# Narrow matmuls of a hybrid decoder trunk laid on alternating column halves of TensorE

## The chip, the cores and the metric

The kernel runs on one core of a Trainium2 chip. The metric is the device time of one execution in microseconds (us). Times come from repeated executions, and one further execution was recorded by the hardware profiler; all rows below are of that one.

## The reference, cut to what matters

One decoder layer for 512 positions, width 1024, all float32. A combined projection of the normalised input feeds three token mixers (sparse attention, spatial gating, RWKV-7), whose outputs are merged and projected. Three small pieces of it are touched here.

```python
# compression of keys and of values (kv = 0, 1): 31 windows of 32 positions, two groups
blk = kv[:, idx] + pe[:, None, :]
hid = silu(einsum('bnlgd,ldh->bngh', blk, w1))        # the first layer
out = einsum('bngh,hd->bngd', hid, w2)
# RWKV-7, 8 heads of 64 channels
kk = kkf / maximum(sqrt(sum(kkf * kkf, axis=-1)), 1e-12)   # a sum of squares per position and head
state = state * d_t + sa * b_t + v_t * k_t                 # the recurrence
y = einsum('bhij,bhj->bhi', state, r_t)                    # its output
y = (y - mean(y)) * rsqrt(var(y) + GN_EPS) * lnx_g + lnx_b # normalised per position and head
```

## The kernel before, in words

Large projections are made with operands split into a high and a low part (`wload` at lines 68 to 79 loads a block of weights, ScalarE makes the high part `wh`, GpSimd or VectorE the low part `wl`); three matmuls into `mm_ps` per piece of the contraction stand for one. These are the bulk of TensorE's work, and they run all the way through. The touched pieces are plain float32 matmuls, each of which is two instructions in the trace; a transpose is one.

All loops are unrolled in Python. The framework orders the instructions of each engine when the kernel is built: it goes by its own estimate of when operands are ready, and among ready instructions takes the one that stands first in the program. On the chip each engine then runs its list in that order.

* First compression layer (loop over `kv` from line 286): 16 matmuls accumulate into `hid`, 64 partitions high, once for keys and once for values. The stationary operand is `blk[:, l, :]` (128 rows by 64 columns), the moving one `w1t[:, l, :]` (128 columns). `hid` has one buffer, so the values' group comes after the keys' result has been read. Each group is followed by tanh, a product, a transpose (`slp`) and the second layer (`pk`).
* Sums of squares (lines 375 to 377): for each of 4 position tiles and 4 channel tiles a matmul with 128x128 stationary columns of `sq` and 8 moving columns of `hind`, into `ss_ps`.
* The recurrence, 8 chunks of 64 positions (`c`, from line 529). Heads lie in 4 pairs `q` with parity `e`; `own[e]` is partitions 0 to 63 or 64 to 127. Per chunk there are 8 matmuls each for `r_ps`, `u_ps` and `st_ps`, whose outputs go to `own[e]` with `e` alternating, and two sets of 8 for the output `Yp`: one of 64x64 operands (from `rt`, whose rows are `own[e]`), one of 128 rows (from `Gt`). Before the change `Yp` is one tile per head parity, and both sets of a chunk write the partition half `ur` that belongs to the chunk's parity `u`.
* Every second chunk the output of two chunks is normalised (`mu`, `yc`, `ysq`, `va`) and transposed by 4 TensorE transposes of 128x128 into `yt_ps`, from which `vt` is updated.

Projections of other parts (`su`, `sv`, `sz`, `sg`, `rz`, `nz`) stand later in the program and fill TensorE between the steps of the recurrence; `canch` (last output matmul of each chunk) anchors two of them.

Of the kernel before, what the change touches and what calls it, by code (L numbers as in the profile page):

```python
# [9 lines left out]
F32 = mybir.dt.float32  # L10
R = mybir.dt.float32r
BF = mybir.dt.bfloat16
AF = mybir.ActivationFunctionType
OP = mybir.AluOpType
AX = mybir.AxisListType
# [29 lines left out]
def hybrid_kernel(ctx, tc, x, p, norm_g, w_in, cmp_w1, cmp_w2, cmp_pe, sg_ln_g, sg_ln_b, sg_w, sg_b,  # L45
# [3 lines left out]
    V, S, G, PE, SY = nc.vector, nc.scalar, nc.gpsimd, nc.tensor, nc.sync  # L49
    x, p, w_in = x[0], p[0, 0], w_in[0]  # L50
# [9 lines left out]
    def mm(o, a, b, start, stop, **kw):  # L60
        return PE.matmul(o, a, b, start=start, stop=stop, **kw).ins  # L61
# [31 lines left out]
    ident = const.tile([128, 128], F32, name="ident")  # L93
# [28 lines left out]
    mhalf = const.tile([128, 32], F32, name="mhalf")  # L122
# [5 lines left out]
    hind = const.tile([128, 4, 8], F32, name="hind")  # L128
# [81 lines left out]
    for t in range(4):  # L210
# [6 lines left out]
        for a in range(2):  # L217
            ks = slice(4 * a, 4 * a + 4)
            ps = xps.tile([128, 4, 128], F32, tag="xt", name="xt_ps")
# [10 lines left out]
    kt_, rt = AR[:, 0], AR[:, 1]  # L230
# [13 lines left out]
    cpp = cp_ctx.enter_context(tc.tile_pool(name="cpp", bufs=1))  # L244
    cps = cp_ctx.enter_context(tc.tile_pool(name="cps", bufs=1, space=PSUM))
# [5 lines left out]
    for half in range(2):  # L251
        c0 = half * 256
        for kv in range(2):
            hs, ls = wkc[kv]
            ps = pmm.tile([128, 512], F32, tag="mm", name="mm_ps")
# [27 lines left out]
    for kv in range(2):  # L283
        for d in range(2):
            SY.dma_start(w2t[:, kv, d * 64:d * 64 + 64], cmp_w2[0, kv])
    for kv in range(2):
        w1t = cpp.tile([128, 16, 128], F32, tag="w1t", name="w1t", bufs=2)
        for lh in range(2):
            SY.dma_start(w1t[lh * 64:lh * 64 + 64], cmp_w1[0, kv, lh * 16:lh * 16 + 16].rearrange("l d h -> d l h"))
        blk = cpp.tile([128, 16, 64], F32, tag="blk", name="blk", bufs=2)  # L290
        src = kc2[:, kv].rearrange("p g (n l) -> p l (g n)", l=16)
        V.tensor_tensor(blk, src, pc("pe", kv * 16, 16).unsqueeze(2).to_broadcast([128, 16, 64]), OP.add)
        hid = cps.tile([64, 128], F32, tag="hid", name="hid")
        for l in range(16):
            mm(hid, blk[:, l, :], w1t[:, l, :], l == 0, l == 15)
        th = cpp.tile([64, 128], F32, tag="th", name="th")
        S.activation(th, hid, AF.Tanh, scale=0.5)
        V.scalar_tensor_tensor(th, th, 1.0, hid, op0=OP.add, op1=OP.mult)
        slp = cps.tile([128, 64], F32, tag="slp", name="slp")
        PE.transpose(slp, th, ident[0:64, 0:64])  # L300
        sl = cpp.tile([128, 2, 4, 32], F32, tag="sl", name="sl")
        if kv == 0:
            sl = sl[:, 0, 0:2, :].rearrange("p g n -> p (g n)")
            V.tensor_copy(sl, slp)
            pk = cps.tile([128, 64], F32, tag="pk", name="pk")
            mm(pk, w2t[:, 0, :], sl, True, True)
            pk2 = pk.rearrange("p (g n) -> p g n", g=2)
            S.activation(kcst[:, :, 0, :], pk2, AF.Copy, scale=0.5)
            V.scalar_tensor_tensor(kcst[:, :, 1, :], pk2, 0.5, f(kcst[:, :, 0, :]), op0=OP.mult, op1=OP.subtract)
        else:  # L310
            V.tensor_copy(sl, slp.rearrange("p (g n) -> p g n", g=2).unsqueeze(2).to_broadcast([128, 2, 4, 32]))
            for g in range(2):
                pk = cps.tile([128, 64], F32, tag="pk", name="pk")
                mm(pk, sl[:, g].rearrange("p a n -> p (a n)"), w2t[:, 1, 0:64], True, True)
                S.activation(vcst[:, g, 0:64], pk, AF.Copy, scale=0.5)
                V.scalar_tensor_tensor(vcst[:, g, 64:128], pk, 0.5, f(vcst[:, g, 0:64]),
                                       op0=OP.mult, op1=OP.subtract)
# [25 lines left out]
    Gt = rp.tile([128, 2, 4, 8, 2, 64], F32, name="Gt")  # L343
    SV = rp.tile([128, 8, 2, 4, 64], F32, name="SV")
# [7 lines left out]
    rps = pr_ctx.enter_context(tc.tile_pool(name="rps", bufs=1, space=PSUM))  # L352
# [4 lines left out]
    for i, src in ((0, rk_w2), (1, rk_a2)):  # L357
        a, o = (slice(0, 64), slice(64, 128)) if i == 0 else (slice(64, 128), slice(0, 64))
# [11 lines left out]
    sqs = []  # L370
# [3 lines left out]
        sqs.append(sq)  # L374
    for t in range(4):
        for q in range(4):
            mm(ss_ps[:, t, :], sqs[q][:, t * 128:(t + 1) * 128], hind[:, q, :], q == 0, q == 3)
    rin = pr.tile([128, 4, 8], F32, name="rin")
    V.tensor_scalar(rin, ss_ps, 1e-24, None, op0=OP.max)
    G.tensor_tensor(rin, rin, mhalf.rearrange("p (a b) -> p a b", b=8), OP.pow)  # L380
# [147 lines left out]
    own = [slice(0, 64), slice(64, 128)]  # L528
    for c in range(8):
        cs = slice(c * 64, c * 64 + 64)  # L530
        u = c % 2
        ur = slice(u * 64, u * 64 + 64)
        if u == 0:
            Yp = [rps.tile([128, 4, 64], F32, tag=f"y{e}", name="Yp") for e in range(2)]
        r_ps = rps.tile([128, 4, 64], F32, tag="ch", name="r_ps", bufs=2)
        for q in range(4):
            for e in range(2):
                mm(r_ps[own[e], q, :], Gt[:, e, q, c, 0, :], SV[:, c, e, q, :], True, True)
        for q in range(4):
            for e in range(2):  # L540
                mm(Yp[e][ur, q, :], rt[own[e], q, cs], SV[own[e], c, e, q, :], q == 0, False,
                   skip_group_check=True)
        r_sb = iv.tile([128, 4, 64], F32, tag="r_sb", name="r_sb", bufs=2)
        S.copy(r_sb, r_ps)
        u_ps = rps.tile([128, 4, 64], F32, tag="ch", name="u_ps", bufs=2)
        for q in range(4):
            for e in range(2):
                mm(u_ps[own[e], q, :], XT[own[e], q * 8 + c, :], r_sb[own[e], q, :], True, True)
        V.tensor_copy(SV[own[0], c, 0], u_ps[own[0]])
        S.copy(SV[own[1], c, 1], u_ps[own[1]])  # L550
        if c < 7:
            s_ps = rps.tile([128, 4, 64], F32, tag="ch", name="st_ps", bufs=2)
            for q in range(4):
                for e in range(2):
                    mm(s_ps[own[e], q, :], BKt[:, c, q, e, :], SV[:, c, e, q, :], True, True)
            tn = iv.tile([128, 4, 64], F32, tag="tn", name="tn", bufs=2)
            dbc = Dt[:, :, c:c + 1].to_broadcast([128, 4, 64])
            if c == 0:
                V.tensor_tensor(tn, s_ps, dbc, OP.mult)
            else:  # L560
                V.tensor_tensor(tn, s_ps, sn, OP.add)
                V.tensor_tensor(tn, tn, dbc, OP.mult)
            sn = tn
            V.tensor_copy(SV[own[0], c + 1, 0], tn[own[0]])
            S.copy(SV[own[1], c + 1, 1], tn[own[1]])
        for q in range(4):
            for e in range(2):
                last = mm(Yp[e][ur, q, :], Gt[:, e, q, c, 1, :], SV[:, c, e, q, :], False, q == 3,
                          skip_group_check=True)
        canch.append(last)  # L570
        if u == 1:
            t = c // 2
            ts = slice(t * 128, (t + 1) * 128)
            mu = iv.tile([128, 4, 2], F32, tag="mu", name="mu", bufs=2)
            yc = iv.tile([128, 4, 2, 64], F32, tag="yc", name="yc", bufs=2)
            for e in range(2):
                V.tensor_reduce(mu[:, :, e], Yp[e], axis=AX.X, op=OP.add)
            V.tensor_scalar(mu, mu, 1.0 / 64, None, op0=OP.mult)
            for e in range(2):
                V.tensor_tensor(yc[:, :, e, :], Yp[e], mu[:, :, e].unsqueeze(2).to_broadcast([128, 4, 64]),  # L580
                                OP.subtract)
            ysq = iv.tile([128, 4, 2, 64], F32, tag="ysq", name="ysq", bufs=1)
            S.activation(ysq, yc, AF.Square)
            va = iv.tile([128, 4, 2], F32, tag="va", name="va", bufs=2)
            V.tensor_reduce(va, ysq, axis=AX.X, op=OP.add)
            V.tensor_scalar(va, va, 1.0 / 64, 64e-5, op0=OP.mult, op1=OP.add)
            G.tensor_tensor(va, va, mhalf[:, 0:8].rearrange("p (a b) -> p a b", b=2), OP.pow)
            V.tensor_tensor(yc, yc, va.unsqueeze(3).to_broadcast([128, 4, 2, 64]), OP.mult)
            ps = rps.tile([128, 4, 128], F32, tag="g", name="yt_ps")
            for q in range(4):  # L590
                PE.transpose(ps[:, q, :], yc[:, q].rearrange("p e i -> p (e i)"), ident)
            for q in range(4):
                V.scalar_tensor_tensor(vt[:, q, ts], ps[:, q, :], pc("lnx_g", q), vt[:, q, ts],
                                       op0=OP.mult, op1=OP.add)
# [391 lines left out]
```

## Time and profile before

| | |
|---|---|
| runs of the kernel, us | 1015.65, 767.99, 767.72 (median 767.99) |
| the profiled execution, us | 766.05 |
| its span, first to last instruction, us | 764.3 |
| TensorE busy, us | 729.1 |
| mean granted TensorE clock | 0.994 |

The profiled execution is 1.75 us longer than its span and 1.94 us shorter than the median. In the timeline rows below the first number is the start in us, the second how long the group of like instructions lasted. Matmuls overlap, so what one costs the engine is read from the distance between starts, not from its duration.

### The profile page before, as it was taken

Reading aid. Unit: us, or ns where it says so; the run is one execution under the profiler, and the core shown is the slowest. Engines: PE = TensorE matmul, PEld = TensorE weight load, DVE = VectorE, ACT = ScalarE, POOL = GpSimd, SP = SyncE. Lnnn points to the kernel's source line nnn. Section 1 sums busy time; section 2 is a strip of 40 time slices with the busy share of each in tenths; the row PEclk is TensorE's granted clock in tenths of the full one; section 3 lists DMA queues with packets and bytes.
Section 4 is the critical chain, followed back from the end, with each engine's and each line's share of the span. In section 5 each row is a group of like instructions: output and inputs, shape, how many; then the busy total and the mean of one; then the engine's idle time right before and its main releaser. Section 6 shows DMA issues by size and latency. Waiting matters only on the chain.

```text
span 764.3 us, 13017 instructions
## 1 busy us (share of the span) xinstructions
PE 729.1 (95%) x4910; PEld 617.9 (81%) x4910; DVE 398.3 (52%) x748; ACT 353.8 (46%) x744; POOL 325.7 (43%) x304
## 2 busy tenths in 40 slices
PE   4899999999999899999899999989999999999996
PEld 4888877899877888778777777867877888998995
DVE  6531387758826642444649455477664222226335
ACT  6455455543362333333456564466654333226453
POOL 6444541120245443423644334534344666255563
PEclk9999999999999999999999999999999999999999
DMA  6843222125535453444533222311116433222222
GB/s 200 189 112 89 56 69 62 36 90 153 147 107 196 112 148 89 115 153 146 155 86 110 70 56 56 82 29 42 42 42 218 141 96 106 88 92 75 84 69 110
DMA packets 106688, 78.71 MB, mean 103 GB/s; under 512 B 5569, under 2 KB 97282, under 8 KB 106626
## 3 DMA queue, kind: packets, MB, share of 16 engines
q1 hardware_dynamic: 105890, 75.27, 34.5%
q10 hardware_dynamic: 736, 2.63, 0.8%
q8 instruction: 38, 0.62, 0.3%
q14 instruction: 24, 0.20, 0.1%
HBM read 67.91 MB, written 9.96 MB: 102 GB/s over the span
## 4 chain that ended last, share of the span: by engine, by line
PE 82%; DVE 7%; DMA 4%; ACT 3%; issue 2%; POOL 1%; SPq 1%; ACTq 0%; POOLq 0%; DVEq 0%
PE mm_ps L61 64%; PE s_ps L61 3%; PE o_ps L61 2%; PE g_ps L61 2%; PE p_ps L850 2%; PE Yp L61 1%; PE hid L61 1%; DMA vn<-dr_sv 1%; DMA xs__129<-in_x_dram 1%; DMA zs<-dr_nz 1%; DVE vn L662 1%; DVE mx L836 1%; ACT wh L77 1%; DVE vn L660 1%; PE mx_ps L61 1%
## 5 line engine op out<-in xcount | busy, mean ns | idle before, releaser
L78 POOL TENSOR_TENSOR wl<-wr,wh 128x512 fp32r<-128x512 f32 (+1 forms) x168 | 224.5, 1344 | 306.4 <-ACT wh L77 288.1
L77 ACT CAST wh<-wr 128x512 fp32r<-128x512 f32 (+1 forms) x194 | 119.3, 620 | 173.9 <-PE mm_ps L61 114.2
L61 PE MATMUL mm_ps<-hH,wh 128*128 128x512 f32 (+1 forms) x440 | 174.4, 396 | 6.4 <-ACT gate L736 2.7
L61 PE MATMUL mm_ps<-hH,wl 128*128 128x512 f32 (+1 forms) x440 | 172.7, 393 | 0.4 <-DVE wl L78 0.4
L61 PE MATMUL mm_ps<-hL,wh 128*128 128x512 f32 (+1 forms) x440 | 172.7, 393 | 0.0
L61 PEld LDWEIGHTS mm_ps<-hH,wh 128*128 128x128 f32 x440 | 83.6, 190 | 25.0 <-ACT gate L736 3.4
L61 PEld LDWEIGHTS mm_ps<-hH,wl 128*128 128x128 f32 x440 | 83.4, 190 | 18.6 <-DVE wl L78 0.6
L61 PEld LDWEIGHTS mm_ps<-hL,wh 128*128 128x128 f32 x440 | 83.4, 190 | 16.9 <-issue 0.4
L61 PE MATMUL mm_ps<-wh,hH 128*128 128x256 f32 (+1 forms) x224 | 64.2, 288 | 4.5 <-DVE st L625 3.3
L61 PE MATMUL mm_ps<-wh,hL 128*128 128x256 f32 (+1 forms) x224 | 64.0, 287 | 0.0
L61 PE MATMUL mm_ps<-wl,hH 128*128 128x256 f32 (+1 forms) x224 | 63.7, 285 | 0.0
L61 PEld LDWEIGHTS mm_ps<-wh,hH 128*128 128x128 f32 x224 | 42.0, 188 | 6.4 <-DVE st L625 3.5
L61 PEld LDWEIGHTS mm_ps<-wl,hH 128*128 128x128 f32 x224 | 42.1, 188 | 0.6
L61 PEld LDWEIGHTS mm_ps<-wh,hL 128*128 128x128 f32 x224 | 42.1, 188 | 0.6 <-issue 0.2
L854 DVE TENSOR_TENSOR pl<-p_ps,ph 128x512 fp32r<-128x512 f32 x40 | 27.1, 684 | 26.8 <-ACT ph L853 26.6
L61 PE MATMUL mm_ps<-ysH,wh 128*128 128x512 f32 x96 | 38.6, 402 | 0.3 <-ACT ysH L705 0.3
L61 PE MATMUL mm_ps<-ysL,wh 128*128 128x512 f32 x96 | 38.4, 400 | 0.2 <-DVE ysL L706 0.2
L61 PE MATMUL mm_ps<-ysH,wl 128*128 128x512 f32 x96 | 38.2, 398 | 0.0
L837 ACT ACTIVATE P<-s_ps,mx 128x512 f32<-128x512 f32 (+3 forms) x64 | 33.4, 531 | 7.9 <-DVE mx L836 5.5
L61 PE MATMUL mm_ps<-wh,mH 128*128 128x256 f32 x128 | 36.2, 287 | 0.6 <-DVE x L899 0.6
L61 PE MATMUL mm_ps<-wl,hT 128*128 128x256 f32 x128 | 35.8, 281 | 0.0
L61 PE MATMUL mm_ps<-wh,hT 128*128 128x256 f32 x128 | 35.8, 285 | 0.0
(336 smaller groups left out, 1450.4 us busy)
## 6 DMA issues: line engine op xcount, KB each, us to landing
wr<-in_w_in_dram SPq DMA_DIRECT2D x130, 256.0 KB
wr<-in_w_branch_dram SPq DMA_DIRECT2D x24, 256.0 KB
wr<-in_w_o_dram SPq DMA_DIRECT2D x16, 256.0 KB
wr<-in_w_ple_gate_dram SPq DMA_DIRECT2D x16, 256.0 KB
xs__129<-in_x_dram SPq DMA_DIRECT2D x4, 512.0 KB
w1t<-in_cmp_w_dram SPq DMA_DIRECT2D x4, 512.0 KB
x<-in_x_dram ACTq DMA_DIRECT2D x4, 512.0 KB
out_dram<-x SPq DMA_DIRECT2D x8, 256.0 KB
```

Of the source, the lines that this page charges most:

```text
L61: return PE.matmul(o, a, b, start=start, stop=stop, **kw).ins
L77: S.copy(h[:, :m], raw[:, :m])
L78: ph_["l"].tensor_tensor(l[:, :m], raw[:, :m], f(h[:, :m]), OP.subtract)
L660: V.tensor_scalar(vn[:, t, :], vn[:, t, :], mv[:, t, 0:1], rs4[:, t:t + 1], op0=OP.subtract, op1=OP.mult)
L662: V.tensor_tensor(vn[:, t, :], vn[:, t, :], lnb, OP.add)
L836: V.tensor_reduce(mx[:, hh:hh + 1], s_ps[:, :W], axis=AX.X, op=OP.max, negate=True)
L837: S.activation(P[:, hh, :W], s_ps[:, :W], AF.Exp, bias=mx[:, hh:hh + 1], accum_out=sm[:, hh:hh + 1])
L850: PE.transpose(p_ps[:, hh * 128:hh * 128 + 128], P[:, hh, kt * 128:kt * 128 + 128], ident)
L854: V.tensor_tensor(pl, p_ps, f(ph), OP.subtract)
```

## The change

The layout of four pieces on TensorE changes, with the layout of the normalisation that follows one of them.

* First compression layer: `hid` is 128 partitions high, keys in the lower half and values in the upper; the two accumulations are interleaved, step by step, in one loop. Tanh and product are done once for both, and one 128x128 transpose takes the place of two. `sl` has a buffer for each.
* Sums of squares: each matmul is cut into two of 64 stationary columns, whose outputs are the lower and the upper partition half of `ss_ps`; 32 matmuls instead of 16.
* Recurrence output: `Yp` is one tile per chunk parity, and the output of a head goes to `own[e]`.
* Transpose of the output: instead of 4 transposes per two chunks, 16 matmuls of 64x64 with a piece of the identity as moving operand.

```diff
-        hid = cps.tile([64, 128], F32, tag="hid", name="hid")
-        for l in range(16):
-            mm(hid, blk[:, l, :], w1t[:, l, :], l == 0, l == 15)
-        th = cpp.tile([64, 128], F32, tag="th", name="th")
-        S.activation(th, hid, AF.Tanh, scale=0.5)
-        V.scalar_tensor_tensor(th, th, 1.0, hid, op0=OP.add, op1=OP.mult)
-        slp = cps.tile([128, 64], F32, tag="slp", name="slp")
-        PE.transpose(slp, th, ident[0:64, 0:64])
-        sl = cpp.tile([128, 2, 4, 32], F32, tag="sl", name="sl")
+        w1.append(w1t)
+        bl.append(blk)
+
+    hid = cps.tile([128, 128], F32, tag="hid", name="hid")
+    for l in range(16):
+        for kv in range(2):
+            mm(hid[kv * 64:kv * 64 + 64], bl[kv][:, l, :], w1[kv][:, l, :], l == 0, l == 15, skip_group_check=True)
+    th = cpp.tile([128, 128], F32, tag="th", name="th")
+    S.activation(th, hid, AF.Tanh, scale=0.5)
+    V.scalar_tensor_tensor(th, th, 1.0, hid, op0=OP.add, op1=OP.mult)
+    slp2 = cps.tile([128, 128], F32, tag="slp", name="slp")
+    PE.transpose(slp2, th, ident)
+    for kv in range(2):
+        slp = slp2[:, kv * 64:kv * 64 + 64]
+        sl = cpp.tile([128, 2, 4, 32], F32, tag=f"sl{kv}", name="sl")
...
-            mm(ss_ps[:, t, :], sqs[q][:, t * 128:(t + 1) * 128], hind[:, q, :], q == 0, q == 3)
+            for u in range(2):
+                mm(ss_ps[u * 64:u * 64 + 64, t, :], sqs[q][:, t * 128 + u * 64:t * 128 + u * 64 + 64], hind[:, q, :],
+                   q == 0, q == 3, skip_group_check=True)
...
-            Yp = [rps.tile([128, 4, 64], F32, tag=f"y{e}", name="Yp") for e in range(2)]
+            Yp = [rps.tile([128, 4, 64], F32, tag=f"y{a}", name="Yp") for a in range(2)]
...
-                mm(Yp[e][ur, q, :], rt[own[e], q, cs], SV[own[e], c, e, q, :], q == 0, False,
+                mm(Yp[u][own[e], q, :], rt[own[e], q, cs], SV[own[e], c, e, q, :], q == 0, False,
                    skip_group_check=True)
...
-                last = mm(Yp[e][ur, q, :], Gt[:, e, q, c, 1, :], SV[:, c, e, q, :], False, q == 3,
+                last = mm(Yp[u][own[e], q, :], Gt[:, e, q, c, 1, :], SV[:, c, e, q, :], False, q == 3,
                           skip_group_check=True)
...
-            mu = iv.tile([128, 4, 2], F32, tag="mu", name="mu", bufs=2)
-            yc = iv.tile([128, 4, 2, 64], F32, tag="yc", name="yc", bufs=2)
-            for e in range(2):
-                V.tensor_reduce(mu[:, :, e], Yp[e], axis=AX.X, op=OP.add)
+            mu = iv.tile([128, 2, 4], F32, tag="mu", name="mu", bufs=2)
+            yc = iv.tile([128, 2, 4, 64], F32, tag="yc", name="yc", bufs=2)
+            for a in range(2):
+                V.tensor_reduce(mu[:, a, :], Yp[a], axis=AX.X, op=OP.add)
...
             for q in range(4):
-                PE.transpose(ps[:, q, :], yc[:, q].rearrange("p e i -> p (e i)"), ident)
+                for a in range(2):
+                    for e in range(2):
+                        mm(ps[own[e], q, a * 64:a * 64 + 64], yc[own[e], a, q, :], ident[own[e], own[e]], True, True)
```

The lines left out change the layouts of `yc`, `ysq` and `va` in the same way, with the same number of instructions of the same sizes.

## Rows read from the trace of the kernel before

**Rows 1.** The page: busy time of each engine.
```profile
PE 729.1 (95%) x4910; PEld 617.9 (81%) x4910; DVE 398.3 (52%) x748; ACT 353.8 (46%) x744; POOL 325.7 (43%) x304
```
**Rows 2.** Windows: stretch, length, busy us of PE, PEld, DVE, ACT, POOL; clock, DMA.
```profile
34.00:46.00 12.00, 12.00 (x72) 9.83 (x71) 4.53 (x7) 5.82 (x11) 4.07 (x4) 1.00 0.89 200
...
240.00:260.00 20.00, 16.66 (x209) 15.33 (x210) 14.96 (x22) 5.85 (x13) 11.65 (x8) 1.00 0.23 62
```
**Rows 3.** Timeline of TensorE in a chunk: two sets that alternate already.
```profile
240.15 0.69 PE L61 MATMUL r_ps<-SV,Gt 128*64 128x64 f32 x16
240.76 0.68 PE L61 MATMUL Yp<-SV,AR 64*64 64x64 f32 x16
241.38 0.38 PE L61 MATMUL mm_ps<-wh,hH 128*128 128x256 f32 x1
```
**Rows 4.** Timeline of TensorE, chunk 4: the 128-row output set and the next group.
```profile
294.58 1.10 PE L61 MATMUL Yp<-SV,Gt 128*64 128x64 f32 x16
295.61 0.70 PE L61 MATMUL mx_ps<-vn,wsT 128*128 128x256 f32 x2
```
**Rows 5.** Timeline of TensorE around the two groups of the first compression layer.
```profile
36.13 3.71 PE L61 MATMUL hid<-w1t,blk 128*64 128x128 f32 x32
39.77 0.51 PE L61 MATMUL mm_ps<-hH,wh 128*128 128x512 f32 x1
...
45.07 0.27 PE L300 MATMUL slp<-ident,th 64*128 64x64 f32 x1
45.27 3.49 PE L61 MATMUL hid<-w1t,blk 128*64 128x128 f32 x30
```
**Rows 6.** Timeline of TensorE: 64-row matmuls with 128 moving columns, alternating and not.
```profile
110.69 1.16 PE L61 MATMUL g_ps<-AR,bk 64*128 64x128 f32 x16
111.78 0.66 PE L467 MATMUL bk_ps<-ident,bk 128*128 128x128 f32 x4
...
120.64 1.16 PE L61 MATMUL g_ps<-AR,bk 64*128 64x128 f32 x8
121.73 0.66 PE L401 MATMUL v_ps<-ident,vt 128*128 128x128 f32 x4
```
**Rows 7.** Timeline of TensorE around the sums of squares.
```profile
70.78 0.73 PE L61 MATMUL ss_ps<-hind,sq 128*128 128x8 f32 x6
71.37 0.60 PE L387 MATMUL hi_ps<-ident,hind 128*8 128x128 f32 x4
...
74.83 2.96 PE L61 MATMUL ss_ps<-hind,sq 128*128 128x8 f32 x26
77.64 0.48 PE L61 MATMUL mm_ps<-hH,wh 128*128 128x512 f32 x1
```
**Rows 8.** Windows just after the sums of squares (columns as in Rows 2).
```profile
79.00:80.00 1.00, 1.00 (x3) 0.74 (x3) 0.00 (x0) 0.00 (x0) 1.00 (x1) 0.50 0.06 18
```
**Rows 9.** Timeline of TensorE around that stretch: first, tenth and eleventh of the large matmuls.
```profile
78.44 0.51 PE L61 MATMUL mm_ps<-hH,wh 128*128 128x512 f32 x1
...
82.08 0.39 PE L61 MATMUL mm_ps<-hH,wh 128*128 128x512 f32 x1
82.31 0.39 PE L61 MATMUL mm_ps<-hL,wh 128*128 128x512 f32 x1
```
**Rows 10.** Timeline of TensorE, last chunk: half of the 64-row output set.
```profile
337.59 0.68 PE L61 MATMUL Yp<-SV,AR 64*64 64x64 f32 x8
338.19 0.66 PE L676 MATMUL ut_ps<-ident,us 128*128 128x128 f32 x4
```
**Rows 11.** Timeline of TensorE: transposes of the output, and the set behind them.
```profile
286.73 0.60 PE L591 MATMUL yt_ps<-ident,yc 128*128 128x128 f32 x4
287.26 0.68 PE L61 MATMUL u_ps<-r_sb,XT 64*64 64x64 f32 x16
287.87 0.70 PE L61 MATMUL mx_ps<-vn,wsT 128*128 128x256 f32 x2
```
**Rows 12.** The chain that ended last: start, length, what.
```profile
225.87 7.13 DMA vn<-dr_sv
```

More of the change, by code (lines that the diff above doesn't have):

```diff
@@ L285, in hybrid_kernel @@
             SY.dma_start(w2t[:, kv, d * 64:d * 64 + 64], cmp_w2[0, kv])
+    w1, bl = [], []
     for kv in range(2):
@@ L531, in hybrid_kernel @@
         u = c % 2
-        ur = slice(u * 64, u * 64 + 64)
         if u == 0:
-            Yp = [rps.tile([128, 4, 64], F32, tag=f"y{e}", name="Yp") for e in range(2)]
+            Yp = [rps.tile([128, 4, 64], F32, tag=f"y{a}", name="Yp") for a in range(2)]
         r_ps = rps.tile([128, 4, 64], F32, tag="ch", name="r_ps", bufs=2)
@@ L573, in hybrid_kernel @@
             ts = slice(t * 128, (t + 1) * 128)
-            mu = iv.tile([128, 4, 2], F32, tag="mu", name="mu", bufs=2)
-            yc = iv.tile([128, 4, 2, 64], F32, tag="yc", name="yc", bufs=2)
-            for e in range(2):
-                V.tensor_reduce(mu[:, :, e], Yp[e], axis=AX.X, op=OP.add)
+            mu = iv.tile([128, 2, 4], F32, tag="mu", name="mu", bufs=2)
+            yc = iv.tile([128, 2, 4, 64], F32, tag="yc", name="yc", bufs=2)
+            for a in range(2):
+                V.tensor_reduce(mu[:, a, :], Yp[a], axis=AX.X, op=OP.add)
             V.tensor_scalar(mu, mu, 1.0 / 64, None, op0=OP.mult)
-            for e in range(2):
-                V.tensor_tensor(yc[:, :, e, :], Yp[e], mu[:, :, e].unsqueeze(2).to_broadcast([128, 4, 64]),
+            for a in range(2):
+                V.tensor_tensor(yc[:, a], Yp[a], mu[:, a, :].unsqueeze(2).to_broadcast([128, 4, 64]),
                                 OP.subtract)
-            ysq = iv.tile([128, 4, 2, 64], F32, tag="ysq", name="ysq", bufs=1)
+            ysq = iv.tile([128, 2, 4, 64], F32, tag="ysq", name="ysq", bufs=1)
             S.activation(ysq, yc, AF.Square)
-            va = iv.tile([128, 4, 2], F32, tag="va", name="va", bufs=2)
+            va = iv.tile([128, 2, 4], F32, tag="va", name="va", bufs=2)
             V.tensor_reduce(va, ysq, axis=AX.X, op=OP.add)
             V.tensor_scalar(va, va, 1.0 / 64, 64e-5, op0=OP.mult, op1=OP.add)
-            G.tensor_tensor(va, va, mhalf[:, 0:8].rearrange("p (a b) -> p a b", b=2), OP.pow)
-            V.tensor_tensor(yc, yc, va.unsqueeze(3).to_broadcast([128, 4, 2, 64]), OP.mult)
+            G.tensor_tensor(va, va, mhalf[:, 0:8].rearrange("p (a b) -> p a b", b=4), OP.pow)
+            V.tensor_tensor(yc, yc, va.unsqueeze(3).to_broadcast([128, 2, 4, 64]), OP.mult)
             ps = rps.tile([128, 4, 128], F32, tag="g", name="yt_ps")
             for q in range(4):
-                PE.transpose(ps[:, q, :], yc[:, q].rearrange("p e i -> p (e i)"), ident)
+                for a in range(2):
+                    for e in range(2):
+                        mm(ps[own[e], q, a * 64:a * 64 + 64], yc[own[e], a, q, :], ident[own[e], own[e]], True, True)
             for q in range(4):
```

## The prediction

> **What bounds the kernel now.** The page comes first: TensorE is busy for 729.1 of 764.3 us [rows 1]. So time taken off it counts unless it falls ahead of a place where TensorE waits for something else. The windows show where that is: from 34 to 46 us it is busy in all of the 12 us, from 240 to 260 us in 16.66 of 20 [rows 2]. In the first stretch a shorter group of matmuls lets the next large matmul start earlier; in the second, what is gained just ahead of the gap becomes waiting. Then come timelines of TensorE for each touched group. There I take the distance from a group's first start to the start of the group behind it, over its instructions. A float32 matmul is two of them.
>
> **What alternating is worth.** Two prices come from the chunks. The set r_ps has 128 rows, 64 stationary and 64 moving columns, with outputs on alternating halves: 240.15 to 240.76 for 16, or 38 ns each [rows 3]. The second output set has the same operand sizes, but all its outputs lie in one half: 294.58 to 295.61 for 16, or 64 ns [rows 4].
>
> **First compression layer.** 64 instructions before and after. Its first group of 32 takes from 36.13 to 39.77, 114 ns each [rows 5], and two such groups are 7.3 us. No row shows 128 moving columns on alternating column halves. The bounds: half of 114, 57 ns, if the halves overlap entirely, and 114 if not at all. In between, the nearest row is g_ps, 64 rows with 128 moving columns: 68 ns where the row halves alternate (110.69 to 111.78 for 16), 136 where they do not (120.64 to 121.73 for 8) [rows 6]. There alternating halves the price, and r_ps against the output set gives 38/64, which makes 68 of the 114. I take 63, between 57 and 68: 64 x 63 ns = 4.0 us, a gain of 3.3 (3.7 to 2.9, and 0 at the far bound). One transpose less saves about the 0.2 us from 45.07 to 45.27 [rows 5]. The keys' group now waits for the values' operands too. That costs nothing as long as large matmuls are ready to fill in: TensorE has no idle time there [rows 2]. If that cover ran out, up to the 3.6 us of one group would be waited for.
>
> **Sums of squares.** 6 instructions take 70.78 to 71.37 and 26 take 74.83 to 77.64 [rows 7], together 3.40 us, or 106 ns each with only 8 moving columns, so the load of 128 stationary columns sets the price. The change makes 64 instructions with half the columns. At r_ps's 38 ns that is 2.4 us; if the halves' loads followed one another, 64 x 53 = 3.4 us and no gain. I take 2.5, a gain of 0.9, because r_ps at 38 ns [rows 3] already loads 64 columns per instruction faster than 53. The Trainium skill has a rule against this, in "TensorE: Matmul & The Clock Gate", Part 3, "The mechanism": a weight load overlaps with matmuls in flight only when the row group differs. With the load time of its Part 2 (columns / 1.2 ns), 64 loads would by estimate take 64 x 53 ns = 3.4 us, no gain here; r_ps, all of one row group, disagrees with it.
>
> Just behind, the granted clock is 0.50, the 1.2 GHz level [rows 8], and nine gaps between large matmuls take 78.44 to 82.08, 3.64 us, against 9 x 0.23 at the full level [rows 9]: 1.5 us lost after groups with hardly any moving columns. With a shorter and denser group this may go away, or not; I leave it out of the sum and put 1.5 us on the low side of the range.
>
> **Recurrence output.** The 128-row set goes from 64 to 38 ns: 16 x 26 ns = 0.42 us a chunk, 3.4 us over 8 chunks. The 64-row set is at 38 to 39 ns already (240.76 to 241.38 [rows 3]), since its row halves alternate. In the last chunk, though, two blocks of 8 stand apart at 75 ns each (337.59 to 338.19 [rows 10], and one more like it): with one tile for both parities they should alternate again, 1.2 down to 0.6 us, a gain of 0.6. Reductions and products on VectorE keep number and size.
>
> **Transposes of the output.** This goes the other way. 4 transposes take 286.73 to 287.26, 0.53 us. Their successors are 16 matmuls, 32 instructions of 64x64. The set u_ps behind them has this size and output halves that alternate with the row halves: 287.26 to 287.87 for 16, 38 ns [rows 11]. At that price they take 1.22 us: a loss of 0.69, four times, 2.8 us. The bounds are 38 ns and the 75 of blocks that do not alternate [rows 10], a loss of 7.5.
>
> **Sum.** -3.3 -0.2 -0.9 -3.4 -0.6 +2.8 = -5.6 us of TensorE time. The 0.4 of chunk 0 falls ahead of the gap between 240 and 260 us and is lost there. That leaves -5.2 on the path: 766.05 becomes 760.9 for an execution like the profiled one, and with the 1.94 us by which the median lies above it, **762.8 us**.
>
> **Rivals.** *Gain swallowed at the next gap.* Three of the terms (-4.4 us) lie before 80 us. At 225.87 the chain runs for 7.13 us through transfers of vn [rows 12]. If something that does not follow TensorE sets their start, the 4.4 us are lost there, and 0.8 remain: 767.2. For it speaks the length of that piece; against it, that the chain reaches it through TensorE's own matmuls and vn is read back from what the kernel itself wrote earlier.
>
> *Column halves overlap only with few moving columns.* Then the first layer and the sums keep their prices, and the Yp terms and the transposes remain: -0.2 -3.4 -0.6 +2.8 +0.4 = -1.0, 767.0. For it: no row shows the new shapes. Against it: r_ps, and g_ps for wide moving operands on row halves. By the rule cited above the loads would not overlap either, which the trace of r_ps does not bear out.
>
> *The halves do not stay alternate (slower).* The planner orders instructions by readiness: g_ps falls apart into blocks at 136 ns [rows 6], the output set at 75 [rows 10]. If it sorted the new groups by half too, the first layer stays at 114 ns (0), the sums run at 64 ns (64 x 64 = 4.1 us, +0.7), the 128-row set stays at 64 (0), the 64-row set goes to 75 in the seven other chunks (0.6 each, +4.2), and the transposes cost 32 x 75 = 2.4 us (+1.9 each, +7.5). With -0.2 that is +12.2 us: 780. It turns slower from the point where the transposes and one more group fall apart. Against it: the blocks that fall apart write two tiles, one per parity, while r_ps and u_ps, one tile each, stay alternate. ss_ps shows why: after 6 instructions it stops [rows 7], although the pieces of the next position tile from the same three channel tiles were ready. So within one tile the order of the program is kept, and after the change each group writes one tile.
>
> A new order of other work, since the planner sees other lengths, could move a few us either way.
>
> **Chances.** The forecast 0.62 (757 to 765: with the clock term, 1.5, the first layer's 0.4 and some 3 us of new order on the low side, 2 on the high), swallowed 0.15, narrow only 0.13, not alternate 0.10. The range takes in the first three: **757 to 768**, leaving out the last and some of the tails. About 2% is what a measurement of this kernel can tell from no change, 15 us, so nearly all cases count as the same: faster 0.03, same 0.93, slower 0.04 (the last rival with a bad new order on top).
>
> **What would show it.** In the changed trace: hid as one run of 64 instructions at 57 to 68 ns; ss_ps at about 38 ns per instruction and perhaps no 0.50 stretch behind it; Yp from Gt at 38 ns in all chunks; yt_ps as 32 instructions in 1.2 us. The piece of the chain at vn should start about 4.4 us earlier; if it starts as before, the gain was swallowed. The prediction is wrong if any of the four prices is that of the same half, or if gaps of TensorE elsewhere grow by more than some 3 us.

## The result and the profile after

| | before | after |
|---|---|---|
| median, us (four runs each) | 768.43 | 759.08 (757.54 to 760.40) |
| ratio, 95% interval | | 0.9876 [0.9847, 0.9904] |
| the profiled execution, us | 766.05 | 759.87 |
| its span, us | 764.3 | 758.2 |
| its mean granted TensorE clock | 0.994 | 0.990 |

The change makes the kernel faster by 1.2%: the ratio leaves out the run of 1015.65 us, which still stands in the median of 768.43, and against 767.99, before's median without it, the gain is 8.9 us. The forecast was 762.8 in 757 to 768: sign and range are right, the gain is 3.7 us larger than forecast. The two profiled executions differ by less, 6.2 us. The part on the clock comes back to that.

The page, the line that answers to [rows 1]:

```profile
PE 721.1 (95%) x5053; PEld 611.6 (81%) x5053; DVE 398.1 (53%) x747; ACT 353.1 (47%) x743; POOL 326.4 (43%) x304
```

TensorE is busy for 8.0 us less, with 143 instructions more. Its timeline after the change, at the five places that answer to [rows 4, 5, 7, 10, 11]: start, length, what.

```profile
36.15 0.43 PE L61 MATMUL hid<-w1t,blk 128*64 128x128 f32 x2
...
39.38 3.68 PE L61 MATMUL hid<-w1t,blk 128*64 128x128 f32 x62 [0.75 <-DMA w1t<-in_cmp_w_dram]
42.99 0.50 PE L61 MATMUL mm_ps<-hH,wl 128*128 128x512 f32 x1
...
71.55 2.04 PE L61 MATMUL ss_ps<-hind,sq 128*64 128x8 f32 x64
73.52 0.49 PE L396 MATMUL hi_ps<-ident,hind 128*8 128x128 f32 x3
...
285.05 1.15 PE L61 MATMUL yt_ps<-ident,yc 64*64 64x64 f32 x32
286.04 0.57 PE L61 MATMUL u_ps<-r_sb,XT 64*64 64x64 f32 x14
...
292.63 0.64 PE L61 MATMUL Yp<-SV,Gt 128*64 128x64 f32 x16
293.19 0.48 PE L61 MATMUL mx_ps<-vn,wsT 128*128 128x256 f32 x1
...
331.85 0.68 PE L61 MATMUL Yp<-SV,AR 64*64 64x64 f32 x16
332.46 0.55 PE L686 MATMUL ut_ps<-ident,us 128*128 128x128 f32 x3
```

From start to start: hid takes 58 ns per instruction (39.38 to 42.99 for 62; before 114), ss_ps 31 (71.55 to 73.52 for 64), the 128-row output set 35 (292.63 to 293.19 for 16; before 64), its 64-row set in the last chunk one run of 0.61 us instead of two of 0.60, and the transposes 31 (285.05 to 286.04 for 32, 0.99 us where four transposes took 0.53). TensorE stands still for 0.75 us before hid, until the values' operand w1t has landed.

Windows of after: length, busy us of PE, PEld, DVE, ACT, POOL; clock, DMA. The first and fourth answer to [rows 2], the second covers the place of [rows 8].

```profile
34.00:46.00 12.00, 11.25 (x95) 9.04 (x94) 3.46 (x4) 4.92 (x9) 3.77 (x3) 1.00 0.83 184
...
78.00:80.00 2.00, 2.00 (x11) 1.59 (x10) 0.15 (x1) 1.39 (x3) 2.00 (x2) 1.00 0.00 0
...
217.00:221.00 4.00, 4.00 (x16) 3.18 (x15) 0.68 (x1) 2.09 (x4) 2.05 (x2) 0.57 0.60 167
...
240.00:260.00 20.00, 19.24 (x231) 18.16 (x232) 11.24 (x22) 7.17 (x17) 11.42 (x8) 0.91 0.29 82
...
241.00:245.00 4.00, 4.00 (x45) 3.77 (x41) 2.84 (x4) 1.01 (x3) 3.78 (x2) 0.57 0.17 66
```

The stretch at the 1.2 GHz level behind ss_ps is gone (clock 1.00 from 78 to 80 us). Others are there, at 217 to 221 and 241 to 245. The chain that ended last can be followed back only to 343.8 us in this trace, so it has no row that answers to [rows 12]; the waits show the stage instead. TensorE's waits between 213 and 256 us, after (us in total, times, longest):

```profile
PE r_ps L61 <- DVE SV L572: 4.3, 1, 4.3
PE st_ps L61 <- DVE SV L557: 1.3, 1, 1.3
PE iv_ps L61 <- ACT Xl L521: 0.7, 1, 0.7
```

and before, same stretch:

```profile
PE mm_ps L61 <- DVE st L625: 3.3, 1, 3.3
PE st_ps L61 <- DVE SV L549: 0.8, 1, 0.8
PE iv_ps L61 <- ACT Xl L512: 0.4, 1, 0.4
```

The gap is still there, 6.3 us instead of 4.5, and TensorE now waits for another instruction. VectorE's timeline in after says why:

```profile
234.58 4.77 DVE L670 TENSOR_SCALAR vn<-vn,mv,rs 128x512 f32<-128x512 f32 x4 [1.19 <-POOL rs L668]
239.27 0.41 DVE L567 TENSOR_TENSOR tn<-st_ps,Dt 128x256 f32<-128x256 f32 x1
...
239.93 0.68 DVE L572 COPY SV<-tn 64x256 f32<-64x256 f32 x1
```

and in before:

```profile
238.71 0.41 DVE L559 TENSOR_TENSOR tn<-st_ps,Dt 128x256 f32<-128x256 f32 x1
239.15 0.28 DVE L564 COPY SV<-tn 64x256 f32<-64x256 f32 x1
239.92 4.80 DVE L660 TENSOR_SCALAR vn<-vn,mv,rs 128x512 f32<-128x512 f32 x4 [0.48 <-POOL rs L658]
```

Before, tn and the state copy ran just ahead of the four normalisations of vn; after, the normalisations come first, and chunk 1's r_ps waits for the copy behind them. Chunk 0 starts 5.9 us earlier than before (r_ps at 213.4 against 219.3 us), chunk 1's r_ps at 240.8 against 240.15, and the output set of chunk 1 ends at 250.3 against 252.7. So this stage took 3.5 us longer.

The queue has a second such place, further ahead. VectorE stands still until the first transfer of vn lands, and chunk 0's copy of u_ps, for which st_ps waits, is in the queue behind the statistics of vn. After:

```profile
229.08 0.69 DVE L664 BATCH_NORM_STATS2 bs<-vn 128x6 f32<-128x512 f32 x1 [11.25 <-DMA vn<-dr_sv]
...
230.63 0.40 DVE L557 COPY SV<-u_ps 64x256 f32<-64x256 f32 x1
```

Before, the same wait is 9.67 us, the statistics start at 233.12 and the copy at 233.95. So the transfer landed 4.0 us earlier after the change, where chunk 0 started 5.9 us earlier.

### The profile page after: what moved, and what is told of

Its sections match the earlier page's. It is cut to its first block, busy times and chain, and to the rows that moved or that the text cites. A ratio compares the mean times of both kernels' runs of the same rounds, so it can differ in the third digit from the quotient of the medians.

```text
span 758.2 us, 13296 instructions
## 1 busy us (share of the span) xinstructions
PE 721.1 (95%) x5053; PEld 611.6 (81%) x5053; DVE 398.1 (53%) x747; ACT 353.1 (47%) x743; POOL 326.4 (43%) x304
## 4 chain that ended last, share of the span: by engine, by line
PE 44%; DVE 5%; DMA 2%; ACT 2%; issue 1%; POOL 0%; ACTq 0%; SPq 0%; POOLq 0%; DVEq 0%
PE mm_ps L61 37%; PE s_ps L61 3%; PE o_ps L61 2%; PE p_ps L860 2%; DMA zs<-dr_nz 1%; DVE mx L846 1%; DVE vt L729 1%; DVE pl L864 1%; DVE ysL L716 1%; DVE pl L832 0%; DMA dr_nz<-st 0%; PE sc_c L61 0%; DMA zs<-dr_rz 0%; DMA zs<-dr_y 0%; DVE nsaY L885 0%
## 5 line engine op out<-in xcount | busy, mean ns | idle before, releaser
L61 PE MATMUL mm_ps<-wl,mH 128*128 128x256 f32 x128 | 35.8, 281 | 0.0
```

## The experiments

Two theories stood after the result. One: alternating halves are worth what the rows say, the stage of vn then swallows most of what was gained ahead of it, and the rest is the granted clock. Two: the layout itself is worth little, and the gain comes from shorter and other groups of instructions or from a new order of the rest. The four kernels of the first batch ran on one chip (before 767.94 us there), the four of the second on another (before 768.36).

**The parts alone.** Each kernel is the one before with one part of the change:

```diff
# p_first: the first layer alone
+            mm(hid[kv * 64:kv * 64 + 64], bl[kv][:, l, :], w1[kv][:, l, :], l == 0, l == 15, skip_group_check=True)
# p_sums: the sums of squares alone
+            for u in range(2):
+                mm(ss_ps[u * 64:u * 64 + 64, t, :], sqs[q][:, t * 128 + u * 64:t * 128 + u * 64 + 64], hind[:, q, :],
# p_yp: output and transposes alone
+                last = mm(Yp[u][own[e], q, :], Gt[:, e, q, c, 1, :], SV[:, c, e, q, :], False, q == 3,
...
+                        mm(ps[own[e], q, a * 64:a * 64 + 64], yc[own[e], a, q, :], ident[own[e], own[e]], True, True)
```

p_first. Expected:

> The kernel before with the first compression layer changed alone. Theory (each group has its own TensorE price and the prices add): hid runs as 62 to 64 instructions at 58 ns, 3.6 to 3.7 us instead of 7.4, and one transpose less; some 3.4 us of TensorE time, so the start of the recurrence comes about 3 us earlier and the whole 1 to 3.5 us faster (ratio 0.995 to 0.999), less where the stage of vn gives it back. Rival (the gain is a matter of the new order of other work): hid gets its price, but the total moves by something unrelated to 3.4 us, by over 4 us in either direction.

Measured: 767.10 us, ratio 0.9994 [0.9972, 1.0016], so no difference that can be told, where 1 to 3.5 us were expected, although hid takes 3.97 us as in after (7.42 before). Chunk 0 starts at 216.2, 3.1 us earlier than before; chunk 1's output ends at 254.0, 1.3 us later. TensorE's waits between 213 and 256 us:

```profile
PE st_ps L61 <- DVE SV L556: 3.2, 1, 3.2
PE r_ps L61 <- DVE SV L571: 2.9, 1, 2.9
```

p_sums. Expected:

> The kernel before with the sums of squares halved alone. Theory: 64 instructions at 31 ns, 2.0 us instead of 3.4, and the stretch at half the granted clock right behind it (78 to 82 us, some 1.5 us lost) goes away: 1.4 to 2.9 us faster up to there. Rival: the clock's fall has nothing to do with this group, then it stays at the same place and only 1.4 us are gained there.

Measured: 768.45 us, 0.9994 [0.9975, 1.0013]. The timeline of its sums (start, length, what):

```profile
70.87 0.52 PE L61 MATMUL ss_ps<-hind,sq 128*64 128x8 f32 x12
71.32 0.60 PE L389 MATMUL hi_ps<-ident,hind 128*8 128x128 f32 x4
...
75.11 1.69 PE L61 MATMUL ss_ps<-hind,sq 128*64 128x8 f32 x52
76.73 0.50 PE L61 MATMUL mm_ps<-hL,wh 128*128 128x512 f32 x1
```

0.45 and 1.62, together 2.07 us for 64, so the sums gain 1.3 us even in two pieces. The granted clock is 1.00 from 76 to 84 us: the stretch at the lower level behind the sums is gone, as the theory had it. That is one execution, and b_vn2 (below), whose sums are those of before, has 1.00 there too. Chunk 0 starts at 217.0, 2.3 us earlier than before; chunk 1's output ends at 252.4, 0.3 us before that of before.

p_yp. Expected:

> The kernel before with the recurrence output and its transposes changed alone. Theory: the 128-row set goes from 64 to 35 ns per instruction in each chunk (-0.47 us x 8), the blocks of the last chunk alternate (-0.6), the transposes cost 0.46 us more each time (+1.8): about 2.5 us faster, all of it after 230 us. Rival (order): the first 215 us are equal, and the stage from 230 to 250 us moves by more than 1 us because VectorE now reduces the first of two chunks early.

Measured: 766.07 us, 0.9969 [0.9950, 0.9987], 1.9 us where about 2.5 were expected. The transposes take 4.12 us in all, as in after; the 128-row and the 64-row output set take 44 and 38 ns per instruction on average over the chunks (64 and 46 before). In its trace chunk 0 starts 1.6 us later than before (220.9 us), ahead of anything that was changed, so this execution does not decide about the rival.

**The same instructions, one half first.** a_rows is the changed kernel with only the order of its loops turned, so that each group goes through one half and then the other:

```diff
-    for l in range(16):
-        for kv in range(2):
+    for kv in range(2):
+        for l in range(16):
...
-    for t in range(4):
-        for q in range(4):
-            for u in range(2):
+    for u in range(2):
+        for t in range(4):
+            for q in range(4):
...
-        for q in range(4):
-            for e in range(2):
+        for e in range(2):
+            for q in range(4):
...
-            for q in range(4):
-                for a in range(2):
-                    for e in range(2):
+            for e in range(2):
+                for q in range(4):
+                    for a in range(2):
```

> The changed kernel with the same instructions, but in each of the four groups all instructions of one half first and then those of the other (the 64-row output set left as it is). Theory (the price comes from alternating): hid at 114 ns (+3.5 us), ss_ps at 53 to 64 ns (+1.4 to +2.1), the 128-row output set at 64 (+3.7), the transposes' successors at 64 to 75 (+4.2 to +5.6): 13 to 15 us slower than the changed kernel, slower than the kernel before by 3 to 6. Rival (the price comes from fewer columns per load and from operand sizes): the same time as the changed kernel within 1 us.

Measured: 767.51 us, 0.9989 [0.9972, 1.0005]: nearly all of the gain is gone. Its timeline at the four groups:

```profile
36.11 6.82 PE L61 MATMUL hid<-w1t,blk 128*64 128x128 f32 x64
42.86 0.50 PE L61 MATMUL mm_ps<-hH,wh 128*128 128x512 f32 x1
...
72.30 2.99 PE L61 MATMUL ss_ps<-hind,sq 128*64 128x8 f32 x52
75.22 0.50 PE L61 MATMUL mm_ps<-hL,wh 128*128 128x512 f32 x1
...
286.13 1.79 PE L61 MATMUL yt_ps<-ident,yc 64*64 64x64 f32 x31
287.70 0.27 PE L61 MATMUL u_ps<-r_sb,XT 64*64 64x64 f32 x1
...
294.49 0.92 PE L61 MATMUL Yp<-SV,Gt 128*64 128x64 f32 x16
295.34 0.70 PE L61 MATMUL mx_ps<-vn,wsT 128*128 128x256 f32 x2
```

hid 105 ns, ss_ps 56, yt_ps 51, Yp 53 per instruction, where after has 58, 31, 31 and 35. Over the whole trace the four groups take 24.5 us against 15.25, 9.3 us more, and the time is 8.4 us longer than after's median. So it is the alternating that gives the groups their prices: the instructions are the same, only their order differs. Writing to another place is not enough. In a_rows each matmul of Yp and yt_ps still writes to a place of its own, and they cost 53 and 51. Three of my four prices for one half were too high (the sums lay within theirs), and the 13 to 15 us with them.

That 8.4 lies so near 9.3 is partly chance. By the table below 2.6 of the 8.4 us are the clock. And the stage of vn is not the same: TensorE waits 3.7 us there in a_rows against 6.3 in after, and VectorE has the state copy (237.08 us) ahead of the normalisations (238.56). Of the second theory a small part stands: g_ps, which the change does not touch, takes 14.68 us in all in after and 15.53 before, in fewer and longer blocks, and a_rows has the same 14.68.

**Vn's work put behind the recurrence on VectorE.** In a_vn2 and b_vn2 (the changed kernel and the one before) the statistics of vn are issued on VectorE only behind chunk 0's copy of u_ps, and each tile's normalisation behind the state copy of one of chunks 0 to 3, with GpSimd's product that goes with it. No operation is added or left out.

```diff
+    svc, svu = [], []
...
+        svu.append(V.tensor_copy(SV[own[0], c, 0], u_ps[own[0]]).ins)
...
+            svc.append(V.tensor_copy(SV[own[0], c + 1, 0], tn[own[0]]).ins)
...
+        with tc.issue_after(svu[0]):
+            V.bn_stats(bs, vn[:, t, :])
+            V.bn_aggr(mv[:, t, :], bs)
...
+        with tc.issue_after(svc[t]):
+            V.tensor_scalar(vn[:, t, :], vn[:, t, :], mv[:, t, 0:1], rs4[:, t:t + 1], op0=OP.subtract, op1=OP.mult)
+            G.tensor_tensor(vn[:, t, :], vn[:, t, :], lng, OP.mult)
+            V.tensor_tensor(vn[:, t, :], vn[:, t, :], lnb, OP.add)
```

a_vn2 and b_vn2, with the changed kernel run once more beside them (after2) and the first layer and the sums without the rest (p_two). Expected of a_vn2:

> The changed kernel with VectorE's work on vn put behind steps of the recurrence: its statistics behind the first chunk's copy of u_ps, and the normalisation of each of the four position tiles behind the state copy of chunks 0 to 3. Theory (what the groups gained ahead of 215 us is given back between 215 and 250 us because the recurrence's copies queue behind vn's work on VectorE): TensorE's waits there (1.3 and 4.3 us in the changed kernel) go away, and the kernel is 3 to 6 us faster than the changed one. Rival (the stage ends when the transfers of vn and the weights land, whatever VectorE's order): the waits move to another place in the same stretch and the time stays within 1.5 us.

Of b_vn2:

> The kernel before with the same two edits to VectorE's order and nothing else. Theory: its waits of 0.8 and 3.3 us in that stretch go away too, 2 to 5 us faster than before; the changed kernel with these edits is then faster than this one by the whole sum of TensorE prices, 8 to 10 us. Rival: no difference from the kernel before.

Of after2:

> The changed kernel once more, as the measure for the others of this call. Both theories: ratio to the kernel before 0.987 to 0.991.

Of p_two:

> The kernel before with the first layer and the sums of squares changed together, the recurrence as before. Theory (upstream gains add, the stage of vn takes 2 to 5 us of them once): the recurrence starts 5 to 6 us earlier than in the kernel before, the end comes 1 to 3 us earlier (ratio 0.996 to 0.999). Rival (the stage takes whatever comes early): no gain at all, ratio 1.000 within 0.002.

Measured: a_vn2 **754.22 us**, 0.9813 [0.9785, 0.9842]; b_vn2 761.83, 0.9914 [0.9884, 0.9944]; after2 759.89, 0.9882 [0.9857, 0.9908]; p_two 764.72, 0.9949 [0.9929, 0.9969]. a_vn2 beats both kernels; against after2 it is 5.7 us shorter. VectorE's timeline in a_vn2 has the old order back, with one normalisation behind the state copy instead of four ahead of it. And chunk 0's copy of u_ps starts 8.1 us earlier than in after, before the first transfer of vn lands:

```profile
222.51 0.42 DVE L558 COPY SV<-u_ps 64x256 f32<-64x256 f32 x1 [4.98 <-PE u_ps L61]
...
233.82 0.41 DVE L568 TENSOR_TENSOR tn<-st_ps,Dt 128x256 f32<-128x256 f32 x1
234.26 0.28 DVE L573 COPY SV<-tn 64x256 f32<-64x256 f32 x1
...
235.03 0.55 DVE L673 TENSOR_SCALAR vn<-vn,mv,rs 128x512 f32<-128x512 f32 x1
```

Its largest wait of TensorE between 213 and 256 us, then that of b_vn2, then p_two's two:

```profile
PE r_ps L61 <- DVE SV L573: 2.8, 1, 2.8
```

```profile
PE r_ps L61 <- DVE SV L565: 1.2, 1, 1.2
```

```profile
PE r_ps L61 <- DVE SV L573: 4.4, 1, 4.4
PE st_ps L61 <- DVE SV L558: 1.8, 1, 1.8
```

With the smaller waits, TensorE waits 3.5 us in this stretch in a_vn2 (6.3 in after) and 1.6 in b_vn2 (4.5 before). So the waits do not go away as expected, they shrink by 2.8 and 2.9 us, and both kernels gain about the same, 5.7 and 6.5 us. The stage is a cost that the kernel before has too. The gain is larger than these waits; where the rest of it lies was not taken apart, and what the statistics and what the normalisations are worth was not run apart either.

The anchored pair differs by 7.6 us, less than the 8 to 10 expected, and the plain pair of that batch by 8.5. Each ratio is known to some 2 us, so the two differences are the same within the noise. The pair does not show that the stage stopped taking its share: a_vn2 still waits 1.9 us longer there than b_vn2, after 1.8 us longer than before.

p_two gains 3.6 us, more than the 1 to 3 expected. It waits 6.9 us in this stretch, with the 0.7 of iv_ps, against 4.5 before.

**The clock in all of it.** Every run comes with the mean granted clock of its span. Time less span x (1 - clock) is an estimate of the time at the full clock; it counts all of the lower level as lost, also where TensorE only waited, and the clock has three digits, so it is good to some 1 us.

| kernel | runs | median, us | mean clock | at the full clock, us |
|---|---|---|---|---|
| before, both chips | 51 | 768.28 | 0.9885 | 759.2 |
| p_first | 12 | 767.10 | 0.9858 | 756.8 |
| p_sums | 12 | 768.45 | 0.9885 | 758.9 |
| p_yp | 12 | 766.07 | 0.9882 | 757.1 |
| p_two | 11 | 764.72 | 0.9868 | 754.1 |
| a_rows | 12 | 767.51 | 0.9883 | 758.7 |
| after and after2 | 10 | 759.78 | 0.9917 | 752.9 |
| b_vn2 | 6 | 761.83 | 0.9907 | 754.8 |
| a_vn2 | 6 | 754.22 | 0.9925 | 749.3 |

Of 8.5 us between before and after in the medians, 6.3 are there at the full clock, and the other two or so are the clock, 0.9885 against 0.9917. The formula takes off somewhat too much: a straight line through the 51 runs of before rises by 0.58 us for each 0.001 that the clock falls, where the formula takes 0.77. With 0.58 the clock's share is 1.9 us, and 6.6 are left. Before's profiled execution has 0.994, near the top of what its runs show (0.982 to 0.995), which fits with the profiled pair differing by 6.2 us only.

## Why the prediction was right

**TensorE bounds the kernel, and its rows give the size.** Summed over all instructions from each start to the next, the touched groups went from before to after: hid 7.42 to 3.97 us (-3.45, forecast -3.3), ss_ps 3.40 to 1.97 (-1.4, forecast -0.9), the 128-row output set 8.23 to 5.19 (-3.0, forecast -3.4), its 64-row set 5.88 to 5.48 (-0.4, forecast -0.6), the transposes 2.00 to 4.12 (+2.1, forecast +2.8), one transpose less 0.41 to 0.03 (-0.4, forecast -0.2). That is -6.6 against -5.6. With the 0.75 us for which hid waits it is -5.8, and at equal clock the runs gained 6.3 to 6.6. The account is not closed by that: the 1.8 us of longer waiting at vn should come off, the 0.85 of g_ps should be added, and some 1.5 us of the gain are then assigned to nothing.

**Prices per instruction.** In the places shown all four lie below the value that I took. The first layer came to 58 ns, at the edge of 57 to 68: with 128 moving columns column halves overlap nearly whole, better than the 68 ns of the row halves of g_ps that I leaned on [rows 6]. For the sums and the transposes r_ps's 38 ns [rows 3] was an upper end; 31 and 31 came out. The 128-row output set has 35 ns in the chunk shown, but 41 on average: in some chunks it is broken up, and in the last it took 58 (334.38 to 335.31 us for 16), as in a_rows. So the sign that I named, 38 ns in all chunks, did not hold there.

By the rule of the Trainium skill ("TensorE: Matmul & The Clock Gate", Part 3, "The mechanism") that a weight load overlaps only where the row group differs, ss_ps would have taken 3.4 us by my estimate from the page's load time. It took 1.97, with all loads over the same 128 rows; a_rows, the same instructions without alternating column halves, has 3.51. Here the measurement decides against the rule.

**The keys' group waits for the values' operands.** I put this at nothing under the cover of large matmuls. The cover ran out by 0.75 us in the profiled execution (0.5 in p_first's and a_vn2's, 0.3 in p_two's, not at all in after2's).

**Rivals.** *The halves don't stay alternate*: hid and ss_ps are runs of 62 and 64 instructions, and the transposes of the chunk shown one of 32; within one tile the program's order was kept, and a_rows shows what the other outcome would have cost. *Column halves overlap only with few moving columns*: hid at 58 ns refutes it. *Gain swallowed at the next gap*: in the profiled pair it looks like it, 3.5 of 5.9 us gone at vn. The reason that I gave, transfers that do not follow TensorE, is not the one: the first transfer landed 4.0 us earlier, near the 4.4 that I named as the sign. But it lags chunk 0 by 1.9 us, and VectorE's queue holds the copy of u_ps behind it; and r_ps's wait of 4.3 us comes from the normalisations ahead of the state copy. Of the 3.5 us, 1.8 are longer waiting; the two stretches at a clock of 0.57 lie in that stage and could be as much as 3.4 us (8 us x 0.43). How much of it stays lost at the end is open. At the full clock p_first and p_sums gain 2.4 and 0.3 us where their rows give 3.3 (3.8 less the 0.5 for which hid waits) and 1.3, but p_two gains 5.1 where its rows give 5.0 (5.3 less 0.3), and the table is good to 1 us. *A new order of other work*: g_ps shows 0.85 us of it.

**The step that was mis-sized** is the end of the sum, "an execution like the profiled one, and with the 1.94 us by which the median lies above it". The 1.94 us carries the mean clock of before over to the changed kernel, and the clock term of 1.5 us stood only on the low side of the range. The changed kernel's runs have 0.9917 instead of 0.9885, about 2 of the 3.7 us by which the forecast was too high; the groups' prices are another 1.0. The stretch behind ss_ps is in fact gone. But the clock is a mean over many runs, and between kernels that differ little it moved by 2 to 3 us of time, with p_first below before. One more such place has the same instructions and waits. Before (start, length, what):

```profile
564.64 0.45 PE L61 MATMUL o_ps<-pl,vcst 128*64 128x512 f32 x1 [1.18 <-DVE pl L822]
...
567.39 0.63 PE L61 MATMUL mm_ps<-hH,wh 128*128 128x512 f32 x1
567.82 0.63 PE L61 MATMUL mm_ps<-hL,wh 128*128 128x512 f32 x1
```

and the same instructions in after:

```profile
559.40 0.45 PE L61 MATMUL o_ps<-pl,vcst 128*64 128x512 f32 x1 [1.18 <-DVE pl L832]
...
561.84 0.39 PE L61 MATMUL mm_ps<-hH,wh 128*128 128x512 f32 x1
562.07 0.39 PE L61 MATMUL mm_ps<-hL,wh 128*128 128x512 f32 x1
```

The same wait of 1.18 us stands ahead of both. Before, the large matmuls start 0.43 us apart, the 1.2 GHz level, after, 0.23. Why one falls and the other does not stays open: no run here changed the clock alone. It does go with the kernels, though. Of the ten traces the seven without all of the alternating groups (before, the four parts, a_rows, b_vn2) show the lower level at this place, and after, after2 and a_vn2 do not. At or just behind the sums it is there in three of the four traces with the group of before, and in none of the six with the halved one. Each trace is one execution, so this is a pattern and not a cause.

## What to carry to other kernels

Where a group of small float32 matmuls writes to one half of TensorE's columns, let consecutive instructions alternate the halves: here that took 105 to 58 ns with 128 moving columns and 51 to 56 down to 31 to 35 with 64 or fewer, with nothing but the order of the loops changed. Take terms from the rows, but look ahead for the next place where the engine waits, and there for the order in which the waiting engine's queue stands: parts gained little or nothing alone (0.9994 twice), and putting vn's statistics and normalisations behind the recurrence's copies on VectorE was worth 5.7 us beside the change's own 8.5 in that batch. Before a profiled run is taken as the kernel, its granted clock is set beside that of the other runs.

## What the runs showed of the hardware

* 64x64 matmuls on alternating diagonal quarters take 31 to 34 ns per instruction, and 128-row ones with 8 moving columns on alternating column halves 31. I had expected r_ps's 38 as the limit. On the quarters row halves alternate too, so they do not show what column halves do alone; the 128-row groups do.
* Column halves alternate at 58 ns with 128 moving columns, 105 without alternating: almost an exact halving.
* VectorE keeps the order of its queue while it waits: in after it stood 11.25 us at statistics whose transfer had not landed, and u_ps, which TensorE had finished at 224.3 us, was copied only behind them, at 230.63. With the copy ahead of the statistics, in a_vn2, it starts at 222.51, right behind u_ps (222.5).
* The clock's lower level comes and goes at unchanged instructions and waits (0.43 against 0.23 us between large matmuls behind the same 1.18 us wait; in seven of ten traces the one, in three the other), and the mean over a span went from 0.982 to 0.995 between runs of one kernel.
